# Seams of a transformer kernel: weight buffers 2/5/5, six feed-forward and five output layers in halves, state space preparation one layer on, other counts for the norm steps

## The chip, the cores and the metric

The kernel runs on one core of one Trainium2 chip. The metric is the device time of one execution in microseconds (us). The engines are PE (TensorE, matmuls), DVE (VectorE), ACT (ScalarE), POOL (GpSimd) and SP (SyncE, which here only issues DMAs). Each engine executes its own instructions in the order written for it, and waits at an instruction until the data and the buffer of that instruction are ready.

## The reference, cut to what matters

Two residual blocks over x of 512 tokens and 1024 features, in fp32, follow one another. Each sublayer starts with a root mean square norm; in the first block each ends with one, too.

```
for layer in range(2):                                     # first block
    hf = swiglu(rms_norm(x, g[0]), w_gate0, w_up0, w_down0)      # ffn0, ffn2
    x = x + 0.5 * rms_norm(hf, g[1])
    xn = rms_norm(x, g[2])
    mix = attn_mixer(xn) if layer == 0 else mlstm_mixer(xn)      # attention, mLSTM
    x = x + rms_norm(mix, g[3])
    hf = swiglu(rms_norm(x, g[4]), w_gate1, w_up1, w_down1)      # ffn1, ffn3
    x = x + 0.5 * rms_norm(hf, g[5])
x = x + even_mixer(rms_norm(x, even_norm))                 # pooling + state space (S5)
x = x + odd_mixer(rms_norm(x, odd_norm))                   # gated convolution of 31 taps
return rms_norm(x, final_norm)

rms_norm(x, g) = x * rsqrt(mean(x * x) + 1e-6) * g
swiglu(x)      = (silu(x @ w_gate) * (x @ w_up)) @ w_down  # 1024 -> 2 x 2816 -> 1024
```

The state space part of the even mixer needs exp(ssm_log_dt), powers of exp(a * dt) and tables made from them; all of that depends on weights alone, not on x.

## The kernel before, in words

x lies transposed in SBUF, as eight tiles x0 to x7 of 128 features by 512 tokens. A projection ("layer", class `Lin`) makes 128 output features: `wload` (L260) loads a 128x1024 weight tile `wt` by a DMA on SP's queue, ACT casts it to the rounded high part `wh` (L267), DVE or POOL subtracts to get the low part `wl` (L268), and `mm3` (L279) sums three matmuls for each of eight input tiles (L287 to L289: wl*xh, wh*xl, wh*xh), 24 matmuls of 512 columns for a layer. `LinTok` (L338) does the same with tokens on the rows (L354 to L356). `wt`, `wh` and `wl` have four buffers each, twelve tiles in all. The inputs are split too: `xs` holds a high part made by ACT (L433) and a low part made by DVE (L434).

A norm is not applied before a projection. The raw x (times the gain) is projected, and the result is multiplied by the factor of each token when it leaves PSUM. The factor is made on the side by `norm_factor` (L444): squares on ACT (L415), sums on POOL and DVE (L417, L419), a matmul with ones (L372) for the sum over features, a small DVE step (L391), a power on POOL (L392, the program name is `rc`, or `rsv` for a norm at a sublayer's end), and a matmul that broadcasts it (L380). These steps are a Python generator (`Chain`), and its next step is emitted after so many groups of three matmuls (`tick`, L179): the numbers that the generators yield (`lag`, 26 in `prenorm`; 6 before L380) say how many groups later.

At a seam between two sublayers the tokens are taken in two halves of 256. The last `ntail` layers of the old sublayer and the first `nfront` of the new one run on the first half and then on the second (`halves`, L316), so that norm and residual of one half (`PostNorm.chain`, L502: L508 scales, L510 reloads the residual `old` from HBM, L512 adds, then L433/L434 split and L415 to L419 square) run beside matmuls of the other. With more layers in halves than `fkeep` = `tkeep` = 4, the weights of the first ones are loaded twice. `ffn` (L516) has four front layers and two tail layers in halves; the output projections of attention (L775) and mLSTM (L1017) have three tail layers.

ffn3 carries a side job: `ssm_prep` (L1055), a generator that is stepped once after each of its undivided layers. Its first step loads ssm_log_dt into `pdt` by two broadcast DMAs (L1066), takes Exp on ACT (L1068) and loads other small arrays.

The order on each engine is made by a tile scheduler from the emitted program, priorities (`ahead`) and buffer waits, so a change of a count moves instructions on all engines.

## Time and profile before

| what | value |
|---|---|
| median of 3 runs | 2602.49 us (2600.59 to 2605.08) |
| profiled execution, its own time | 2600.32 us |
| its span, first to last instruction | 2597.8 us |
| mean granted TensorE clock | 0.982 |
| PE busy | 2469.4 us, 95% of the span, 12816 instructions |
| DVE / ACT / POOL busy | 1353.9 / 1043.9 / 645.5 us |
| HBM traffic | 101 GB/s over the span |

The sublayers follow one another: ffn0 to about 385 us, attention to 690, ffn1 to 1055, ffn2 to 1440, mLSTM to 1718, ffn3 to 2120, the even mixer to 2330, the odd mixer to 2530, the output and final norm to the end. PE's busy time is to be read with care: matmuls overlap, so the length of one (0.28 us) is not its cost; the distance between two starts is. Waits in square brackets stand at the instruction that waited, with the engine and line that released it.

### The profile page before, as it was taken

To read this page: it belongs to the slowest core of one execution; us is meant where nothing else is said; L and a number is where in the kernel's file an instruction comes from. 1 tells how busy PE (TensorE), PEld (TensorE's weight loads), DVE (VectorE), ACT (ScalarE), POOL (GpSimd) and SP (SyncE) were. 2 spreads that over 40 slices of the span, in tenths; PEclk is the share of its full clock that TensorE was granted. 3 is DMA by queue.
4 is the path that set the end of the run, shared out by engine and by line. 5 is a ranking of instruction groups with operands and counts; after the bars stand their busy time and mean duration, and the time that the engine had idled before them with its cause. 6 is when DMAs were issued, how large, how long until landed. Compare 5 with 4: busy or idle time off the path is not lost. (4 is left out here: it accounts for less than half of the span.)

```text
span 2597.8 us, 33290 instructions
## 1 busy us (share of the span) xinstructions
PE 2469.4 (95%) x12816; PEld 2071.8 (80%) x12816; DVE 1353.9 (52%) x2288; ACT 1043.9 (40%) x1778; POOL 645.5 (25%) x568
## 2 busy tenths in 40 slices
PE   8999989999999999899999899969999997999887
PEld 7888887677888888888888788868888886787677
DVE  5444246657544422644423567459963255656885
ACT  4222234446522222422223445443232247446762
POOL 2111025030311100211101253022211024317951
PEclk9999999999999999999999999989999999999998
DMA  5223335122432233422333422233433353132211
GB/s 168 96 96 93 97 103 189 49 85 66 146 104 95 95 93 106 154 98 98 95 89 102 139 97 66 86 114 126 162 131 91 95 170 136 51 121 65 65 57 49
DMA packets 99918, 268.91 MB, mean 104 GB/s; under 512 B 17280, under 2 KB 34304, under 8 KB 99248
## 3 DMA queue, kind: packets, MB, share of 16 engines
q1 hardware_dynamic: 99760, 266.79, 32.2%
q8 instruction: 101, 1.65, 0.3%
q14 instruction: 57, 0.47, 0.1%
HBM read 241.56 MB, written 20.99 MB: 101 GB/s over the span
## 5 line engine op out<-in xcount | busy, mean ns | idle before, releaser
L287 PE MATMUL pa<-xs,wl 128*128 128x512 f32 (+1 forms) x2352 | 877.8, 373 | 10.5 <-DVE wl L268 7.6
L288 PE MATMUL pa<-xs,wh 128*128 128x512 f32 (+1 forms) x2352 | 875.6, 372 | 5.1 <-DVE xs L434 5.0
L289 PE MATMUL pa<-xs,wh 128*128 128x512 f32 (+1 forms) x2352 | 872.5, 371 | 0.0
L267 ACT CAST wh<-wt 128x1024 fp32r<-128x1024 f32 (+2 forms) x423 | 432.5, 1023 | 1012.5 <-issue 602.2
L268 DVE TENSOR_TENSOR wl<-wt,wh 128x1024 fp32r<-128x1024 f32 (+2 forms) x369 | 445.7, 1210 | 456.6 <-ACT wh L267 455.5
L287 PEld LDWEIGHTS pa<-xs,wl 128*128 128x128 f32 x2352 | 445.2, 189 | 88.7 <-ACT sq L415 7.1
L288 PEld LDWEIGHTS pa<-xs,wh 128*128 128x128 f32 x2352 | 445.1, 189 | 80.4 <-DVE xs L434 7.0
L289 PEld LDWEIGHTS pa<-xs,wh 128*128 128x128 f32 x2352 | 445.0, 189 | 74.2 <-issue 1.8
L533 POOL TENSOR_TENSOR ew<-ew,rb 128x512 f32<-128x512 f32 (+1 forms) x96 | 160.5, 1673 | 711.5 <-ACT ew L532 711.5
L287 PE MATMUL pa<-hh,wl 128*128 128x512 f32 (+1 forms) x880 | 310.9, 353 | 13.7 <-DVE wl L268 13.7
L288 PE MATMUL pa<-hl,wh 128*128 128x512 f32 (+1 forms) x880 | 308.9, 351 | 0.0
L289 PE MATMUL pa<-hh,wh 128*128 128x512 f32 (+1 forms) x880 | 308.8, 351 | 0.0
L287 PEld LDWEIGHTS pa<-hh,wl 128*128 128x128 f32 x880 | 166.8, 190 | 39.0 <-DVE wl L268 14.8
L493 POOL TENSOR_TENSOR acc<-acc,ew 128x512 f32<-128x512 f32 (+1 forms) x44 | 51.0, 1159 | 546.5 <-ACT ew L488 546.5
L288 PEld LDWEIGHTS pa<-hl,wh 128*128 128x128 f32 x880 | 166.9, 190 | 24.2
L289 PEld LDWEIGHTS pa<-hh,wh 128*128 128x128 f32 x880 | 166.8, 190 | 24.1
L540 DVE TENSOR_TENSOR ew<-ew,pa 128x512 f32<-128x512 f32 (+1 forms) x96 | 61.7, 643 | 228.2 <-PE pa L289 217.0
L268 POOL TENSOR_TENSOR wl<-wt,wh 128x1024 fp32r<-128x1024 f32 x54 | 129.6, 2410 | 124.5 <-ACT wh L267 124.3
L531 DVE TENSOR_TENSOR ew<-rb,pa 128x512 f32<-128x512 f32 (+1 forms) x96 | 61.4, 642 | 176.8 <-PE pa L289 174.9
L1440 POOL TENSOR_TENSOR tp<-tp 128x512 f32<-128x512 f32 x72 | 100.0, 1389 | 5.1 <-ACT tp L1436 0.7
L1447 DVE SCALAR_TENSOR_TENSOR pc<-g,vecs,pc 128x512 f32<-128x512 f32 x120 | 85.8, 751 | 4.4 <-PE pc L1445 3.4
L488 ACT ACTIVATE ew<-pa 128x512 f32<-128x512 f32 (+1 forms) x56 | 27.4, 488 | 139.4 <-PE pa L289 139.4
(455 smaller groups left out, 2915.5 us busy)
## 6 DMA issues: line engine op xcount, KB each, us to landing
wt<-in_wgu_dram SPq DMA_DIRECT2D x176, 512.0 KB, 3.5
wt<-in_wd_dram SPq DMA_DIRECT2D x72, 512.0 KB, 3.5
wt<-in_wd_dram SPq DMA_DIRECT2D x36, 384.0 KB, 3.1
wt<-in_ow_dram SPq DMA_DIRECT2D x24, 512.0 KB, 3.2
old<-x SPq DMA_DIRECT2D x40, 256.0 KB, 3.3
old<-old SPq DMA_DIRECT2D x80, 128.0 KB, 2.5
wt<-in_aqk_dram SPq DMA_DIRECT2D x18, 512.0 KB, 4.2
wt<-in_mvo_dram SPq DMA_DIRECT2D x16, 512.0 KB, 3.6
```

The lines of the kernel that those rows point to most:

```text
L267: nc.scalar.copy(wh, wt)
L268: (eng or nc.vector).tensor_tensor(wl, wt, wh.bitcast(F32), op=ALU.subtract)
L287: mm(ps[:m, c0:c1], wl[:, j, :], xh[:, c0:c1], start=first and j == 0, stop=False)
L288: mm(ps[:m, c0:c1], wh[:, j, :], xl[:, c0:c1], start=False, stop=False)
L289: mm(ps[:m, c0:c1], wh[:, j, :], xh[:, c0:c1], start=False, stop=last and j == n - 1)
L488: nc.scalar.activation(sq[:, c0:c1], ps[:, c0:c1], AF.Square)
L493: eng.tensor_tensor(s.acc[:, c0:c1], s.acc[:, c0:c1], sq[:, c0:c1], op=ALU.add)
L531: nc.vector.tensor_tensor(s[:, c0:c1], rb[:, c0:c1], ps[:, c0:c1], op=ALU.mult)
L533: nc.gpsimd.tensor_tensor(s[:, c0:c1], s[:, c0:c1], rb[:, c0:c1], op=ALU.mult)
L540: nc.vector.tensor_tensor(s[:, c0:c1], s[:, c0:c1], ps[:, c0:c1], op=ALU.mult)
L1440: nc.gpsimd.tensor_tensor(part, part, t, op=ALU.add)
L1447: nc.vector.scalar_tensor_tensor(ps, gi[:, j:j + T], cw[:, at[j]:at[j] + 1], ps, op0=ALU.mult, op1=ALU.add)
```

## The change

Five counts and four orders change.

- `wload`: two buffers for `wt`, five each for `wh` and `wl`; still twelve tiles.
- `norm_factor`: nine groups between power and broadcast, not six. `prenorm`: lag 28 for the first half and 38 for the second, not 26.
- `ffn`: six front layers in halves, not four, in ffn1 to ffn3; two of them are loaded twice. The output projections of attention and mLSTM: five tail layers in halves, not three; one is loaded twice. That is 8 loads more (431 after 423), and 240 matmuls more (10 more layers are cut in two).
- The side job starts after the second undivided layer of ffn3, not the first; that layer is now the eighth of the sublayer.
- The first attention projections and the first value projection subtract `wl` on DVE, not POOL (8 subtracts).
- mLSTM: the gates' matmuls use the other PSUM pool, run by halves, and stand after two of the four token blocks of v; `keep_x` (the residual's copy to HBM) comes later.

```
-    wt = k.wp.tile(shape, F32, name="wt", tag="wt", bufs=4)
+    wt = k.wp.tile(shape, F32, name="wt", tag="wt", bufs=2)
...
-    wh = k.wp.tile(shape, R, name="wh", tag="wh", bufs=4)
-    wl = k.wp.tile(shape, R, name="wl", tag="wl", bufs=4)
+    wh = k.wp.tile(shape, R, name="wh", tag="wh", bufs=5)
+    wl = k.wp.tile(shape, R, name="wl", tag="wl", bufs=5)
...
-    prs = yield from rsqrt_mean(k, t, c0, c1, 1024, 1e-6, 6, v)
+    prs = yield from rsqrt_mean(k, t, c0, c1, 1024, 1e-6, 9, v)
...
-def prenorm(k, g, c0, c1, lag=26, order=range(KX)):
+def prenorm(k, g, c0, c1, lag=None, order=range(KX)):
+    lag = lag or (28 if c0 == 0 else 38)
...
-        run_lins(lins[:4], nfront=4)
+        nf = 4 if begin else 6
+        run_lins(lins[:nf], nfront=nf)
...
-                for l in lins[4:n1]:
+                for n, l in enumerate(lins[nf:n1]):
                     run_lins([l])
-                    next(work, None)
+                    if n:
+                        next(work, None)
...
-            lins = [Lin(k, [(A["aqk"][2 * a + j, i], KX)], xs, ev, nc.gpsimd) for j, ev in ((1, ev_k), (0, ev_q))]
+            eng = None if (a, i) == (0, 0) else nc.gpsimd
+            lins = [Lin(k, [(A["aqk"][2 * a + j, i], KX)], xs, ev, eng) for j, ev in ((1, ev_k), (0, ev_q))]
...
-                lin_tok(k, A["av"][0], xs, ev_v(0), nc.gpsimd)
+                lin_tok(k, A["av"][0], xs, ev_v(0))
...
-        run_lins([Lin(k, [(A["ao"][m], KX)], ys, post.evac(m)) for m in range(KX)], ntail=3, on_half=post.finish)
+        run_lins([Lin(k, [(A["ao"][m], KX)], ys, post.evac(m)) for m in range(KX)], ntail=5, on_half=post.finish)
...
-            pg = k.A_()
-            for c in HALVES:
-                mm3(k, pg, gw, xs, *c)
+            pg = k.S_()
+            mm3(k, pg, gw, xs, *HALVES[0])
+            yield
+            mm3(k, pg, gw, xs, *HALVES[1])
...
-        for tb in range(4):
+        for tb in range(2):
             lv[0].run(tb)
-        k.need("all", 0, T)
-        old = keep_x(k)
         with k.phase("mlstm_a") as pa:
             gt = gates(pa)
+            next(gt)
+            for tb in range(2, 4):
+                lv[0].run(tb)
+            k.need("all", 0, T)
+            old = keep_x(k)
             next(gt)
```

What the scheduler makes of it is shown at three places. Line numbers after the change are a little higher, by one in the norm steps (L508 is L509) up to eight from the state space on (L1068 is L1076).

**ffn0 to attention.** On DVE before, the low part `wl_2791` of a weight tile of ffn0's last layer stands between the splits xs5 and xs6 of the first half:

```order
L434 SCALAR_TENSOR_TENSOR xs4_103<-x4_95,vecs_89,xs4_103 128x256
L434 SCALAR_TENSOR_TENSOR xs5_104<-x5_96,vecs_89,xs5_104 128x256
L268 TENSOR_TENSOR wl_2791<-wt_2788,wh_2790 128x1024
L417 TENSOR_TENSOR ssq_2718<-ssq_2718,sq_2726 128x256
L434 SCALAR_TENSOR_TENSOR xs6_105<-x6_97,vecs_89,xs6_105 128x256
L417 TENSOR_TENSOR ssq_2718<-ssq_2718,sq_2729 128x256
L434 SCALAR_TENSOR_TENSOR xs7_106<-x7_98,vecs_89,xs7_106 128x256
L419 TENSOR_TENSOR ssq_2718<-ssq_2718,ssq_2710 128x256
```

and after the change it stands before the whole residual chain, right behind `wl_2785`:

```order
L268 TENSOR_TENSOR wl_2547<-wt_2544,wh_2546 128x768
L268 TENSOR_TENSOR wl_2785<-wt_2782,wh_2784 128x1024
L268 TENSOR_TENSOR wl_2791<-wt_2788,wh_2790 128x1024
L494 TENSOR_TENSOR acc_1995<-acc_1995,ew_2617 128x256
L391 TENSOR_SCALAR rsv_2636<-pb_2633 128x2
L509 TENSOR_TENSOR ew_2654<-x0_91,pb_2651 128x256
```

So this subtract moved up 24 places, ahead of the chain. On PE before, the sum over features of the second half's squares (L372 on `ssq`) comes when the first two projections (`pt`) have gone through all eight input tiles:

```order
L356 MATMUL pt<-wh,xs_106 128x512
L354 MATMUL pa<-wh,xs_99 128x512
L355 MATMUL pa<-wl,xs_99 128x512
L356 MATMUL pa<-wh,xs_99 128x512
L372 MATMUL pb<-ones,ssq 128x128 x2
L354 MATMUL pa<-wh,xs_100 128x512
L355 MATMUL pa<-wl,xs_100 128x512
```

and after it comes 30 places earlier, when the projections have only gone through the first two tiles and part of the third:

```order
L355 MATMUL pa<-wl,xs_99 128x512
L356 MATMUL pa<-wh,xs_99 128x512
L354 MATMUL pa<-wh,xs_100 128x512
L355 MATMUL pa<-wl,xs_100 128x512
L356 MATMUL pa<-wh,xs_100 128x512
L354 MATMUL pa<-wh,xs_101 128x512
L372 MATMUL pb<-ones,ssq 128x128 x2
L354 MATMUL pa<-wh,xs_99 128x512
L355 MATMUL pa<-wl,xs_99 128x512
L356 MATMUL pa<-wh,xs_99 128x512
```

The order of the two projections and of the value blocks is now mixed, tile by tile.

**ffn1 to ffn2.** On DVE before, the weights of the old sublayer's last layer (`wl_8370`) stand inside the chain of the first half:

```order
L434 SCALAR_TENSOR_TENSOR xs5_104<-x5_96,vecs_89,xs5_104 128x256
L268 TENSOR_TENSOR wl_8370<-wt_8367,wh_8369 128x1024
L417 TENSOR_TENSOR ssq_8297<-ssq_8297,sq_8305 128x256
L434 SCALAR_TENSOR_TENSOR xs6_105<-x6_97,vecs_89,xs6_105 128x256
L417 TENSOR_TENSOR ssq_8297<-ssq_8297,sq_8308 128x256
L434 SCALAR_TENSOR_TENSOR xs7_106<-x7_98,vecs_89,xs7_106 128x256
L419 TENSOR_TENSOR ssq_8297<-ssq_8297,ssq_8289 128x256
L268 TENSOR_TENSOR wl_8376<-wt_8373,wh_8375 128x768
```

and after the change, at the second half's chain of the same seam, the weights `wl_8822` and `wl_8856` of new front layers stand behind the sum of squares (L419) and the last split:

```order
L417 TENSOR_TENSOR ssq_8728<-ssq_8728,sq_8739 128x256
L434 SCALAR_TENSOR_TENSOR xs6_105<-x6_97,vecs_89,xs6_105 128x256
L419 TENSOR_TENSOR ssq_8728<-ssq_8728,ssq_8720 128x256
L434 SCALAR_TENSOR_TENSOR xs7_106<-x7_98,vecs_89,xs7_106 128x256
L541 TENSOR_TENSOR ew_8746<-ew_8746,pa_8756 128x256
L268 TENSOR_TENSOR wl_8822<-wt_8819,wh_8821 128x1024
L276 TENSOR_TENSOR hl0_8602<-ew_8746,hh0_8601 128x256
L268 TENSOR_TENSOR wl_8856<-wt_8853,wh_8855 128x1024
```

Two weight tiles that the matmuls of the front layers need now stand behind the chain.

**mLSTM to ffn3.** On ACT before, the Exp on `pdt` stands directly before the second half's squares (L415) and splits (L433), with its table load:

```order
L488 ACTIVATE ew<-pa 128x256
L489 ACTIVATE x_96<-pa,vecs 128x256
L267 CAST wh<-wt 128x1024
L1068 ACT_TABLE_LOAD
L1068 ACTIVATE pdt<-pdt 128x16
L415 ACTIVATE ssq<-x_91 128x256
L433 ACTIVATE xs_99<-x_91,vecs 128x256
L415 ACTIVATE sq<-x_92 128x256
```

and after the change the first half's broadcast factor (L451) has come ahead of it, but the squares still follow it:

```order
L489 ACTIVATE ew<-pa 128x256
L490 ACTIVATE x_94<-pa,vecs 128x256
L451 COPY rb<-pb 128x256
L267 CAST wh<-wt 128x1024 x2
L1076 ACT_TABLE_LOAD
L1076 ACTIVATE pdt<-pdt 128x16
L415 ACTIVATE ssq<-x_91 128x256
L415 ACTIVATE sq<-x_92 128x256
```

On SP's DMA queue before, the two loads of `pdt` follow five weight loads, the reload of `old` and one small load:

```order
L264 DMA wt<-in_wgu_dram 128x1024 x5
L510 DMA old<-old 128x256 x8
L1062 DMA pa__14061<-in_sa_dram 128x32
L1066 DMA pdt<-in_ldt_dram 64x16x1 x2
L1076 DMA pskip<-in_sd_dram 128x16
L1125 DMA pb__14174<-in_sb_dram 128x2x64
L264 DMA wt<-in_wgu_dram 128x1024
```

and after the change they follow six weight loads, of which two stand directly in front of them:

```order
L264 DMA wt<-in_wgu_dram 128x1024 x2
L511 DMA old<-old 128x256 x8
L264 DMA wt<-in_wgu_dram 128x1024 x2
L1070 DMA pa__14499<-in_sa_dram 128x32
L264 DMA wt<-in_wgu_dram 128x1024 x2
L1074 DMA pdt<-in_ldt_dram 64x16x1 x2
L1084 DMA pskip<-in_sd_dram 128x16
L1133 DMA pb__14613<-in_sb_dram 128x2x64
```

The loads of `pdt` thus moved behind one more weight load, and the last weight loads ahead of them need a free `wt` buffer out of two.

## Rows read from the trace of the kernel before

**Rows 1.** The page: busy time of each engine, share of the span, instructions.

```profile
PE 2469.4 (95%) x12816; PEld 2071.8 (80%) x12816; DVE 1353.9 (52%) x2288; ACT 1043.9 (40%) x1778; POOL 645.5 (25%) x568
```

**Rows 2.** Waits of PE: us in total, times, longest us.

```profile
PE pa L287 <- DVE wl L268: 24.8, 7, 7.2
...
PE pb L380 <- POOL rc L392: 24.2, 9, 18.0
...
PE pb L372 <- DVE ssq L419: 10.7, 3, 5.2
...
PE pe L1291 <- POOL xx L1284: 9.1, 3, 4.3
...
PE pt L355 <- POOL wl L268: 1.7, 1, 1.7
```

**Rows 3.** Groups and DMA issues of the page: busy us, mean ns; KB, us to landing.

```profile
L268 DVE TENSOR_TENSOR wl<-wt,wh 128x1024 fp32r<-128x1024 f32 (+2 forms) x369 | 445.7, 1210 | 456.6 <-ACT wh L267 455.5
...
L268 POOL TENSOR_TENSOR wl<-wt,wh 128x1024 fp32r<-128x1024 f32 x54 | 129.6, 2410 | 124.5 <-ACT wh L267 124.3
...
L267 ACT CAST wh<-wt 128x1024 fp32r<-128x1024 f32 (+2 forms) x423 | 432.5, 1023 | 1012.5 <-issue 602.2
...
wt<-in_wgu_dram SPq DMA_DIRECT2D x176, 512.0 KB, 3.5
```

**Rows 4.** Timeline of PE: matmuls on 256 and on 512 columns, start and length in us.

```profile
1074.06 0.28 PE L287 MATMUL pa<-xs,wl 128*128 128x256 f32 x1
...
1075.74 0.28 PE L289 MATMUL pa<-xs,wh 128*128 128x256 f32 x1
...
1199.79 0.39 PE L287 MATMUL pa<-xs,wl 128*128 128x512 f32 x1
...
1201.15 0.39 PE L287 MATMUL pa<-xs,wl 128*128 128x512 f32 x1
```

**Rows 5.** Timeline of PE, ffn0 to attention, with waits.

```profile
383.29 0.58 PE L287 MATMUL pa<-hh,wl 128*128 128x256 f32 x1 [7.02 <-DVE wl L268]
...
396.93 0.49 PE L380 MATMUL pb<-ident,rsv 128*128 128x128 f32 x2 [1.27 <-POOL rsv L392]
```

**Rows 6.** Timeline of VectorE (DVE) before the wait at 383 us.

```profile
376.97 5.13 DVE L434 SCALAR_TENSOR_TENSOR xs<-x,vecs,xs 128x256 fp32r<-128x256 f32 x2
...
382.02 1.21 DVE L268 TENSOR_TENSOR wl<-wt,wh 128x1024 fp32r<-128x1024 f32 x1
...
383.49 0.47 DVE L434 SCALAR_TENSOR_TENSOR xs<-x,vecs,xs 128x256 fp32r<-128x256 f32 x1
```

**Rows 7.** Timeline of GpSimd (POOL) beside the first row of Rows 6.

```profile
376.98 4.83 POOL L268 TENSOR_TENSOR wl<-wt,wh 128x1024 fp32r<-128x1024 f32 x2 [0.55 <-ACT wh L267]
```

**Rows 8.** Timeline of PE, ffn1 to ffn2.

```profile
1055.42 0.39 PE L287 MATMUL pa<-hh,wl 128*128 128x256 f32 x1 [3.21 <-DVE wl L268]
...
1078.21 0.68 PE L372 MATMUL pb<-ones,ssq 128*128 128x128 f32 x4 [2.20 <-DVE ssq L419]
```

**Rows 9.** Timeline of VectorE, first and last of the second half's chain.

```profile
1067.06 0.75 DVE L508 TENSOR_TENSOR ew<-x,pb 128x256 f32<-128x256 f32 x2 [1.58 <-PE pb L380]
...
1077.65 0.42 DVE L419 TENSOR_TENSOR ssq<-ssq 128x256 f32<-128x256 f32 x1
```

**Rows 10.** Timeline of PE, mLSTM to ffn3.

```profile
1730.74 0.28 PE L289 MATMUL pa<-xs,wh 128*128 128x256 f32 x1
...
1749.05 1.22 PE L380 MATMUL pb<-ident,rc 128*128 128x128 f32 x4 [18.03 <-POOL rc L392]
```

**Rows 11.** Timeline of ScalarE (ACT) in that wait.

```profile
1737.66 1.28 ACT L1068 ACT_TABLE_LOAD   x1 [17.90 <-DMA pdt<-in_ldt_dram]
```

**Rows 12.** Tile pdt: its DMAs, and their time to landing.

```profile
L1066 SPq DMA_DIRECT2D pdt<-in_ldt_dram x2: 653/664/674, 1715.2 to 1715.9; - x2
...
DMA to landing us min/median/max: 12.5/17.1/21.7
```

**Rows 13.** Window after that wait: us, busy of each engine, PEclk, DMA share, GB/s.

```profile
1749.00:1755.00 6.00, 5.89 (x32) 5.60 (x33) 4.29 (x27) 3.54 (x8) 2.38 (x4) 0.64 0.44 137
```

More of the change, by code (lines that the diff above doesn't have):

```diff
@@ L572, in ffn @@
         else:
-            run_lins(lins[4:n1])
+            run_lins(lins[nf:n1])
         pb = late.enter_context(k.phase("ffn_b"))
@@ L1016, in mlstm @@
         post = PostNorm(k, k.vec(9), old)
-        run_lins([Lin(k, [(A["mo"][m], KX)], ys, post.evac(m)) for m in range(KX)], ntail=3, on_half=post.finish)
+        run_lins([Lin(k, [(A["mo"][m], KX)], ys, post.evac(m)) for m in range(KX)], ntail=5, on_half=post.finish)
 def cmul(nc, tmp, o_re, o_im, ar, ai, br, bi, eng=None, sub=None):
```

## The prediction

> **What bounds the kernel now.** I read the busy times of the page first. PE is busy for 2469 of 2597.8 us [rows 1], so the other engines matter only where PE waits for them. The list of PE's waits comes next, and it shows where that is: 24.8 us for weight low parts in 7 waits, 24.2 us for norm factors (one wait alone has 18.0), 10.7 us for sums of squares, 9.1 us for the rotation in the even mixer [rows 2]. Nearly all of these stand at seams, where one sublayer's norm chain and the next one's first weights meet. Third come the timelines of PE around each such wait, and of the engine named as its releaser. The change is about these seams alone; inside the sublayers the order on PE stays as it is or nearly so. The forecast is therefore a sum over seams: which wait goes, and what is late next.
>
> **Prices.** A weight subtract takes 1.21 us on DVE and 2.41 on POOL, a cast 1.02 on ACT, and a 512 KB weight load lands 3.5 us after issue [rows 3]. A matmul on 256 columns takes 0.120 us start to start ((1075.74 - 1074.06) / 14), one on 512 columns 0.227 ((1201.15 - 1199.79) / 6) [rows 4]. A layer cut in halves thus costs 48 x 0.120 - 24 x 0.227 = 0.3 us more than a whole one. Ten more are cut: +3.0 us on PE, which I book at their seams, 0.6 for each pair. Eight more loads of 3.5 us lie beside 5.4 us layers and cost nothing by themselves; if a buffer is late they cost as in the second rival.
>
> **The change part by part,** in the order of the program, after minus before.
>
> *ffn0 to attention: -6.* PE waits 7.0 us at 383.29 for a weight low part [rows 5], because DVE has this subtract behind two splits (L434) of 5.13 us together, where another split takes 0.47 [rows 6]. POOL runs two weight subtracts in the same 5 us [rows 7]. After the change the subtract stands ahead of the chain, so the 7.0 goes. The mixed order of the first projections also covers the 1.27 us at 396.93 [rows 5] and the 1.7 us wait for a POOL subtract [rows 2]: 10.0 in all. But the sum of squares of the second half is now asked for 30 matmuls earlier, 30 x 0.227 = 6.8 us. The chain of a half takes 11 us (below), of which I find some 3.4 uncovered by following both queues: -10.0 + 3.4, rounded to -6. If all the covers hold it is -9; if the chain keeps the slow splits (5.13 - 2 x 0.47 = 4.2 us longer), about -2.
>
> A rule of the Trainium skill bears on this place (SBUF — State Buffer, "Who interferes with whom"): a VectorE instruction with two inputs in SBUF and a GpSimd instruction that reads SBUF shut each other out, and the one that starts first holds the shared ports to its end. The trace agrees here, with 5.13 us for two splits beside 4.83 us of POOL subtracts [rows 6, 7]. By this rule moving the subtracts to DVE takes 4.2 us of blocking out of the chain and puts 2.4 us of subtracts in, so the seam would come out 1.8 us better than my -6; I leave it inside the bounds, since the subtracts also stand in the chain's queue.
>
> *Attention to ffn1: +1.2.* Four more layers in halves; the waits of this seam are for the same chain and stay. Bounds -4 (chain hidden by the longer run in halves) to +4 (two reloads late by one 3.5 us landing).
>
> *ffn1 to ffn2: +2.3.* The 3.21 us wait at 1055.42 [rows 8] goes, since that subtract now stands before the chain. The second half's chain lasts from 1067.06 to 1078.07, 11 us [rows 9], and PE waits 2.20 us for its end at 1078.21 [rows 8]. After the change only two half layers, not three to four, stand between, one half layer (24 x 0.120 = 2.9) less: I get a wait of 4.85, that is +2.65. Then `wl_8822`, which stands behind the chain on DVE, is late by a subtract (1.2 and the step to PE: 1.4), and the next weight by some 0.8. With 0.6 for two layers in halves: -3.2 + 2.65 + 1.4 + 0.8 + 0.6. Bounds -3 (the weights are ready) to +6 (each of four weights behind the chain late by 1.2 more).
>
> *ffn2 to mLSTM: +0.6.* The longest wait for a sum of squares, 5.2 us [rows 2], turns into one for the last split of about 7.2, since the gates' matmuls now come early and ask for the second half; the factors come 1.4 earlier, and 0 to 0.6 are lost behind a cast on ACT that came between table loads. No more is lost than one chain's end, so bounds -3 to +4.
>
> *mLSTM to ffn3: +1.4.* This is the big wait: PE's last matmul before it starts at 1730.74, and the next comes at 1749.05 [rows 10]. It is put down to POOL's `rc`, but POOL and DVE had waited themselves: ACT stood 17.9 us at the Exp of the side job, until 1737.66, for `pdt` [rows 11]. Its two loads of 4 KB, issued at 1715.2 and 1715.9, took 12.5 and 21.7 us to land [rows 12], and all squares and splits of the second half are behind that Exp on ACT. After the change five tail layers let the first factor come 5.8 us earlier and get past the Exp. The squares of the second half do not: the Exp still stands ahead of them. And the loads of `pdt` are now behind one more weight load on SP's queue, which has to wait for one of only two `wt` buffers; I find their issue at about 1722, 6.5 us later, and landing at 1722 + 21.7 = 1744. Eight squares and the sums follow in 6 us, to 1750. PE has four half layers until about 1734.6 in the meantime, and then waits some 15 us instead of 18. But eleven layers are cut in halves at this seam instead of seven, +1.2, and the end of the front comes out at 1776.5 where it was 1775.1. So the change doesn't do here what the moved side job seems to offer. Bounds -10 (first rival) to +8 (`pdt` another 6.5 late).
>
> The Trainium skill (DMA: Bandwidth & Descriptors, "Rules for kernel authors") has a rule against this part: issue a DMA early and wait for it late, and a last dimension that is not contiguous costs a descriptor for each element. The trace agrees, with 21.7 us for 4 KB beside 3.5 us for 512 KB [rows 3, 12]. By the rule the later issue alone would cost the whole 6.5; by the queues above, 5.8 of it is paid back by the earlier factor.
>
> *ffn3 to even: -1.6.* A wait for a weight of 2.2 us, one of the seven [rows 2], goes as in ffn1 to ffn2, less 0.6 for halves already counted in the front. Bounds -3 to 0.
>
> *Even mixer: +2.4.* Before the last pair of rotations POOL now has one more weight subtract in its queue, 2.41 us [rows 3], and PE waits for that rotation already (4.3 us at most [rows 2]). Bounds 0 to 4.8, for none and two.
>
> *Start, odd mixer, output: -1.* At the start the factor comes 3 groups later, and PE has other half layers there (-0.5); the output has four layers to start on where it had three (-0.7); bounds -3 to +2.
>
> Sum: -6 + 1.2 + 2.3 + 0.6 + 1.4 - 1.6 + 2.4 - 1 = -0.7. The profiled execution took 2600.3 us, 2.5 around its span, and lies 2.2 below the median. On that scale I expect 2599.6, on the scale of the median 2602.5 - 0.7 = 2601.8.
>
> **The rivals.**
> First, the 18 us wait goes after all. For it: the factor of the first half does get past the Exp, and the two loads may land in 12.5 us each when less traffic surrounds them. Against it: the Exp's place ahead of the squares. Then PE waits perhaps 5 us for the 11 us chain in place of 18, and the restart is spared as well: in the 6 us after the wait the granted clock was 0.64 [rows 13], between the two levels of 1.2 and 2.4 GHz, a loss of 0.36 x 6 = 2.2 us. -13 - 2.2 gives 2587.
>
> Second, slower: two `wt` buffers starve the halves. A buffer is held for landing, cast and subtract, 3.5 + 1.02 + 1.21 = 5.7 us [rows 3], so two buffers give a weight each 2.9 us, while a half layer takes 2.9 us on PE. There is no slack, and one subtract that is held up behind a chain delays all that follow. It decides once a subtract comes over 3 us late; then each of five seams loses some 2 us more: +10, 2612. Against it: whole layers of 5.4 us win it back, and the converted `wl` and `wh` have one buffer more.
>
> Third, faster at several seams without touching the big wait: the attention seam gives all of its -9, and the weights behind the chains are ready in time (-3 and -3 at the feed-forward seams, 0 in the even mixer): some -9, 2593. For it: 24.8 us of waits for weights is the largest sum in the list. Against it: what stands next in the queues is the 11 us chain, and it is not shorter.
>
> **How the numbers follow.** Forecast as it stands (2596 to 2607): 0.41. First rival 0.16, second 0.22, third 0.21. A measurement of this kernel can tell 0.2%, 5.2 us, from no change. The first and third rival are faster, 0.37; the forecast is the same, 0.41; the second is slower, 0.22. The range from 2586 to 2613 takes in all three rivals' middles and leaves out their far ends.
>
> **What would show it.** Right: the wait of 7 us at 383 is gone and a wait for `ssq` of 3 to 4 us stands in its place; after ffn1 a wait for `ssq` of nearly 5 us, then short ones for `wl`; ACT still waits some 20 us for `pdt`, and PE some 15 in two pieces. Wrong: no wait over 8 us left between 1700 and 1770 (first rival), or a row of `wl` waits of 1 to 3 us after each seam (second).

## The result, and the profile after

The changed kernel took 2624.36 us (median of 4 runs, 2621.32 to 2626.22), the kernel before 2602.09 us beside it: a ratio of 1.0083, 95% interval 1.0066 to 1.0100. It is slower by 22 us, where I had forecast no change (2601.8) and a range to 2613. The profiled execution has a span of 2624.2 us, 26.4 more than before's, and is one of the two slower of its four.

The page's busy times of the changed kernel, as in [rows 1]:

```profile
PE 2476.8 (94%) x13056; PEld 2087.2 (80%) x13056; DVE 1369.7 (52%) x2313; ACT 1055.2 (40%) x1802; POOL 640.5 (24%) x567
```

PE has 7.4 us more work, from 240 matmuls more and from matmuls at a lower clock. The other 19 us are waits. PE's waits in the changed kernel (total, times, longest), as in [rows 2]:

```profile
PE pb L372 <- DVE ssq L419: 17.5, 8, 6.7
PE pa L287 <- DVE ew L532: 17.4, 1, 17.4
PE pe L1299 <- POOL xx L1289: 11.3, 1, 11.3
PE pa L287 <- DVE wl L268: 11.0, 4, 7.2
PE pa L287 <- ACT x L490: 10.3, 3, 4.8
...
PE pa L354 <- DVE vx L876: 6.6, 1, 6.6
...
PE pb L380 <- POOL rc L392: 5.9, 5, 1.9
```

The 24.8 us for weight low parts are down to 11.0, as forecast. But the waits for sums of squares grew from 10.7 to 17.5, a wait of 17.4 us stands where 18.0 stood, under another name (it ends with a split's `ew`, no more with `rc`), and three are new or grown: 11.3 us for one rotation in the even mixer, 10.3 for ACT's copies (L490), 6.6 for a split of v (the L876 row).

Where the time came from is read by the start of the same matmul in both timelines, for instance the first down projection of each feed-forward sublayer, the first and last score matmul of attention, the first pooling matmul of the even mixer. The stretches between them, changed minus before:

| stretch | forecast | measured |
|---|---|---|
| ffn0 to attention | -6 | -3.1 |
| attention to ffn1 | +1.2 | +2.0 |
| ffn1 to ffn2 | +2.3 | +6.4 |
| ffn2 to mLSTM | +0.6 | +3.6 |
| mLSTM to ffn3 | +1.4 | +8.9 |
| ffn3 to even mixer, rotations | +0.8 | +11.6 |
| all the rest | -1 | -3.0 |
| sum | -0.7 | +26.4 |

A measured row is the difference of two single traces, and the granted clock of a stretch differs from execution to execution: in two runs below, c_rest and c_444_lags, PE's waits from ffn0 to attention are the same 6.5 us, and the stretch is 3.8 us apart, with a granted clock of 0.96 and 0.99. So a difference of less than some 4 us between two stretches is not read as a cause unless the waits show it, too.

Three stretches carry it. **The even mixer**: POOL's, ACT's, DVE's and PE's timelines around the third rotation of the changed kernel.

```profile
2214.23 2.40 POOL L268 TENSOR_TENSOR wl<-wt,wh 128x1024 fp32r<-128x1024 f32 x1 [11.28 <-ACT wh L267]
2222.25 4.67 POOL L268 TENSOR_TENSOR wl<-wt,wh 128x1024 fp32r<-128x1024 f32 x2 [5.62 <-ACT wh L267]
2226.87 1.26 POOL L1279 TENSOR_TENSOR r<-r,r 128x512 f32<-128x512 f32 x1
```

```profile
2214.71 6.39 ACT L1303 COPY yf<-pe 32x128 f32<-32x128 f32 x16
2221.12 1.05 ACT L267 CAST wh<-wt 128x1024 fp32r<-128x1024 f32 x1
```

```profile
2213.77 0.68 DVE L1281 TENSOR_TENSOR r<-pe,rot 128x512 f32<-128x512 f32 x1
2228.16 2.27 DVE L1285 TENSOR_TENSOR_SCAN r<-rot,r 128x512 f32<-128x512 f32 x1 [13.71 <-POOL r L1279]
```

```profile
2236.31 0.79 PE L1299 MATMUL pe<-xx,mt 128*128 128x127 f32 x2 [11.26 <-POOL xx L1289]
2241.11 0.80 PE L1299 MATMUL pe<-xx,mt 128*128 128x127 f32 x2 [4.01 <-POOL xx L1292]
```

DVE's products are ready at 2214.4. POOL's addition (L1279) comes at 2226.87, 12.4 us later, since three weight subtracts (7.1 us together) stand ahead of it and the second waits 5.62 us for its cast. (The first one's wait of 11.28 us is over at 2214.23, just before the products are ready.) The cast at 2221.12 in turn stands behind 16 copies of 6.39 us on ACT. PE waits 11.26 and then 4.01 us.

The kernel before waited for its rotations, too: 9.1 us [rows 2], and 3.8 us in this row of the same list.

```profile
PE pe L1291 <- POOL xx L1281: 3.8, 2, 2.0
```

So 15.3 us in two long waits stand in place of 12.9 in five, 2.4 us more. All of PE's waits in this stretch are 31.1 us, 20.3 before: of the other 8.4 us, the input splits have 3.4, ACT's copies to `u` 3.1 and POOL's weights 2.2.

**mLSTM to ffn3**: SP's queue, ACT and PE, as in [rows 10 to 12].

```profile
1731.09 2.08 SPq L264 DMA_DIRECT2D wt<-in_wgu_dram  x2
1733.22 1.39 SPq L1074 DMA_DIRECT2D pdt<-in_ldt_dram  x2
```

```profile
1756.84 1.28 ACT L1076 ACT_TABLE_LOAD   x1 [18.52 <-DMA pdt<-in_ldt_dram]
```

```profile
1763.30 0.58 PE L287 MATMUL pa<-xs,wl 128*128 128x256 f32 x1 [17.44 <-DVE ew L532]
```

The loads of `pdt` go out at 1733.22, right behind two weight loads; the Exp on ACT waits 18.52 us for them until 1756.84, and PE 17.44 us until 1763.30. And ahead of that a wait that the kernel before doesn't have, ACT and PE:

```profile
1718.22 1.29 ACT L433 ACTIVATE xs<-x,vecs 128x256 fp32r<-128x256 f32 x3
...
1719.41 0.36 ACT L489 ACTIVATE ew<-pa 128x256 f32<-128x256 f32 x1
```

```profile
1720.19 0.58 PE L287 MATMUL pa<-yh,wl 128*128 128x256 f32 x1 [4.79 <-ACT x L490]
```

PE has finished a tail layer's second half and needs its PSUM bank, but ACT copies it out (L489, L490) only after the squares and splits of the first half, from 1719.41 on.

**ffn1 to ffn2**: PE at the second half's sum of squares, and the windows behind it and behind the waits of 4.79 and 17.44 us above (length, busy of each engine, PEclk, DMA share, GB/s).

```profile
1077.55 1.19 PE L372 MATMUL pb<-ones,ssq 128*128 128x128 f32 x4 [6.72 <-DVE ssq L419]
```

```profile
1077.40:1082.00 4.60, 3.88 (x16) 3.61 (x17) 3.40 (x6) 0.41 (x1) 0.71 (x1) 0.50 0.64 196
1082.00:1087.00 5.00, 5.00 (x33) 5.00 (x32) 2.09 (x4) 2.40 (x3) 0.00 (x0) 0.69 0.34 103
1720.70:1725.00 4.30, 4.30 (x28) 4.30 (x27) 4.30 (x9) 1.77 (x6) 0.97 (x2) 0.69 0.21 61
1763.30:1768.00 4.70, 4.70 (x23) 4.70 (x24) 4.70 (x11) 4.67 (x11) 1.63 (x1) 0.53 0.97 351
```

The wait is 6.72 us, where [rows 8] have 2.20. In the 4.6 us behind it the clock was granted at 0.50, that is at the lower of its two levels, and at 0.69 in the next 5; behind the waits of 4.79 and 17.44 us shown above it was 0.69 and 0.53. In the same place of the kernel before, behind its wait of 2.2 us, it was full:

```profile
1078.10:1083.00 4.90, 4.74 (x38) 4.61 (x39) 2.90 (x9) 2.23 (x6) 2.12 (x3) 1.00 0.37 107
```

So by my estimate from these rows the long wait costs up to another 4.6 x 0.50 + 5 x 0.31 = 3.9 us.

### The profile page after: what moved, and what is told of

The parts are those of the page before. It is cut to its first block, busy times and chain, and to the rows that moved or that the text cites. A ratio compares the mean times of both kernels' runs of the same rounds, so it can differ in the third digit from the quotient of the medians.

```text
span 2624.2 us, 33843 instructions
## 1 busy us (share of the span) xinstructions
PE 2476.8 (94%) x13056; PEld 2087.2 (80%) x13056; DVE 1369.7 (52%) x2313; ACT 1055.2 (40%) x1802; POOL 640.5 (24%) x567
## 5 line engine op out<-in xcount | busy, mean ns | idle before, releaser
L287 PE MATMUL pa<-xs,wl 128*128 128x512 f32 (+1 forms) x2408 | 889.2, 369 | 35.8 <-DVE ew L532 17.4
L288 PE MATMUL pa<-xs,wh 128*128 128x512 f32 (+1 forms) x2408 | 884.5, 367 | 0.4 <-DVE xs L434 0.4
L289 PE MATMUL pa<-xs,wh 128*128 128x512 f32 (+1 forms) x2408 | 882.0, 366 | 0.0
L267 ACT CAST wh<-wt 128x1024 fp32r<-128x1024 f32 (+2 forms) x431 | 440.8, 1023 | 1053.4 <-issue 485.3
L268 DVE TENSOR_TENSOR wl<-wt,wh 128x1024 fp32r<-128x1024 f32 (+2 forms) x385 | 465.1, 1209 | 466.7 <-ACT wh L267 465.9
L287 PEld LDWEIGHTS pa<-xs,wl 128*128 128x128 f32 x2408 | 458.9, 191 | 111.0 <-DVE ew L532 17.6
L289 PEld LDWEIGHTS pa<-xs,wh 128*128 128x128 f32 x2408 | 458.6, 190 | 72.1 <-issue 2.0
L288 PEld LDWEIGHTS pa<-xs,wh 128*128 128x128 f32 x2408 | 458.9, 191 | 71.6 <-ACT wh L267 1.0
L287 PEld LDWEIGHTS pa<-hh,wl 128*128 128x128 f32 x880 | 165.4, 188 | 24.2
L268 POOL TENSOR_TENSOR wl<-wt,wh 128x1024 fp32r<-128x1024 f32 x46 | 111.0, 2418 | 148.8 <-ACT wh L267 148.6
L489 ACT ACTIVATE ew<-pa 128x256 f32<-128x256 f32 (+1 forms) x60 | 28.0, 466 | 136.4 <-PE pa L289 136.4
```

The lines of the kernel that those rows point to most:

```text
L267: nc.scalar.copy(wh, wt)
L268: (eng or nc.vector).tensor_tensor(wl, wt, wh.bitcast(F32), op=ALU.subtract)
L287: mm(ps[:m, c0:c1], wl[:, j, :], xh[:, c0:c1], start=first and j == 0, stop=False)
L288: mm(ps[:m, c0:c1], wh[:, j, :], xl[:, c0:c1], start=False, stop=False)
L289: mm(ps[:m, c0:c1], wh[:, j, :], xh[:, c0:c1], start=False, stop=last and j == n - 1)
L489: nc.scalar.activation(sq[:, c0:c1], ps[:, c0:c1], AF.Square)
```

## The experiments

"Before" is run beside each, at 2601 to 2603 us. The number after a time is its ratio to "before", and all intervals are 95%. Names such as a_444 are those of the runs; what a stretch gains or loses is given against the kernel before, as in the table above.

**One part of the change undone.** The buffers at 4/4/4:

```
-    wt = k.wp.tile(shape, F32, name="wt", tag="wt", bufs=2)
+    wt = k.wp.tile(shape, F32, name="wt", tag="wt", bufs=4)
-    wh = k.wp.tile(shape, R, name="wh", tag="wh", bufs=5)       (and wl)
+    wh = k.wp.tile(shape, R, name="wh", tag="wh", bufs=4)       (and wl)
```

> The changed kernel with four buffers each for wt, wh and wl again (all other edits stay). Theory: two wt buffers hold back the two weight loads that stand in front of the pdt loads on SP's queue; with four the pdt loads go out near 1722 us instead of 1733, so the stretch from mLSTM to ffn3 gets some 8 us back. The even mixer keeps its loss, since the order on POOL there is the same (four weight subtracts between the second and the third rotation): its segment from ffn3's first down projection to the first pooling matmul stays at 255.7 us within 3. Total about 2614. Rival (the buffers are the cause of all of it): every seam goes back to before, total 2602 to 2605. Second rival (buffers cost nothing): 2624.

Measured (a_444): 2618.34, ratio 1.0063 (1.0048 to 1.0078). Six us come back, but not where I said: the loads of `pdt` do go out earlier, at 1726.0 in place of 1733.2, but PE still waits 18.8 us there and mLSTM to ffn3 stays at +9.3. The even mixer goes from +11.6 to +4.7, and PE's waits in it from 31.1 to 22.4 us. With four buffers two subtracts, as in the kernel before, and no longer four, stand between the second and the third rotation, and POOL adds at once behind them, 4.5 us after DVE's products:

```profile
2209.66 2.39 POOL L268 TENSOR_TENSOR wl<-wt,wh 128x1024 fp32r<-128x1024 f32 x1 [8.73 <-ACT wh L267]
2217.78 2.40 POOL L268 TENSOR_TENSOR wl<-wt,wh 128x1024 fp32r<-128x1024 f32 x1 [5.73 <-ACT wh L267]
2220.14 1.29 POOL L1279 TENSOR_TENSOR r<-r,r 128x512 f32<-128x512 f32 x1
```

The counts of the norm steps:

```
-    prs = yield from rsqrt_mean(k, t, c0, c1, 1024, 1e-6, 9, v)
+    prs = yield from rsqrt_mean(k, t, c0, c1, 1024, 1e-6, 6, v)
-    lag = lag or (28 if c0 == 0 else 38)
+    lag = lag or 26
```

> The changed kernel with the old counts of the norm steps (26 for both halves, 6 before the broadcast), everything else as changed, two wt buffers too. Theory: the counts set the order in the even mixer; with the old ones three weight subtracts stand on POOL before the third rotation in place of four, and the wait of 11.3 us there falls to about 5, some -7; at ffn1 to ffn2 the second sum of squares is asked for later, some -2. Total about 2615. Rival (buffers alone): no change, 2624 within 3.

Measured (a_lags): 2626.26, 1.0098 (1.0083 to 1.0113). No gain in all: the wait of 11.3 us fell to 3.1, but one of 5.2 for ACT's copies came ahead of it, and what ffn2 to mLSTM gained (8 us) ffn0 to attention and attention lost.

Three tail layers in halves, and four front layers (each alone):

```
-        run_lins([Lin(k, [(A["mo"][m], KX)], ... ntail=5, on_half=post.finish)     (A["ao"] too)
+        run_lins([Lin(k, [(A["mo"][m], KX)], ... ntail=3, on_half=post.finish)
...
-        nf = 4 if begin else 6
+        nf = 4
```

> The changed kernel with three tail layers in halves at the output projections of attention and mLSTM. Theory: the two new waits of PE for ACT's copies of a tail layer (4.7 us at 675, 4.8 us at 1720, L490 behind the first half's squares and splits on ACT) come from the five layers in halves and go; the segment to ffn1 falls by some 2 and that to ffn3 by some 4 (less halves 1.2 too); total 2618. Rival: the first half's chain is then uncovered instead and its factor later, no gain or some 4 us of loss.

Measured (b_ntail3): 2620.46, 1.0069 (1.0054 to 1.0084): 4 us. By the traces 2.8 lie at mLSTM to ffn3 and 2.9 in the even mixer, and attention to ffn1 lost 2.7; each is small enough to be the clock of one execution.

> The changed kernel with four front layers in halves in ffn1 to ffn3. Theory: the wait of 6.7 us for the second sum of squares at 1077 comes from the counts and not from the number of front layers, so it stays, and only 0.6 us for each of three seams comes back: 2622. Rival (six layers in halves with two wt buffers starve PE): ffn1 to ffn2 gets 3 to 6 us back and the other seams some 2, total below 2616.

Measured (b_nf4): 2617.12, 1.0056 (1.0041 to 1.0071). The wait for the sum of squares stays (6.4 us), as the theory said, but 7 us come back: 4.3 in the even mixer (1.9 of them in PE's waits), 3.1 at mLSTM to ffn3 (a wait of 2.8 us inside ffn3, for a state space table, is gone), 2.3 at ffn1 to ffn2.

**One part of the change alone.** The kernel before with 2/5/5, with 2/4/4 and with 3/4/4. In these three the edit also gave the same number, 2 or 3 in place of 4, to a tile of attention that has the same name (L703), a part that the change doesn't have:

```
-    wt = k.wp.tile(shape, F32, name="wt", tag="wt", bufs=4)
+    wt = k.wp.tile(shape, F32, name="wt", tag="wt", bufs=2)
-    wh = k.wp.tile(shape, R, name="wh", tag="wh", bufs=4)       (and wl)
+    wh = k.wp.tile(shape, R, name="wh", tag="wh", bufs=5)       (and wl)
...
-            wt = pool.tile([P, T], F32, name="wt", tag="wt", bufs=4)
+            wt = pool.tile([P, T], F32, name="wt", tag="wt", bufs=2)
```

> The kernel before with buffers 2/5/5 and nothing else. Theory: two wt buffers by themselves bring a weight late wherever the next load waits for a subtract that stands in a long queue; the even mixer loses some 7 (as 4/4/4 gave 7 back there in the changed kernel), the start of ffn3 0 to 3; total 2609 to 2612. Rival (the loss needs the halves and the counts too): 2602 within 3.

Measured (b_255): 2624.43, 1.0084 (1.0067 to 1.0101).

> The kernel before with two wt buffers, wh and wl at four as before. Theory: the loss of buffers 2/5/5 comes from the two wt buffers, since a load for the next sublayer can't be issued before an old subtract behind the norm chain is done; the five wh and wl give little back: 2622 to 2630. Rival (the fifth wh and wl changed the order on the engines and did the harm): below 2610.

Measured (c_b244): 2635.26, 1.0126 (1.0109 to 1.0144).

> The kernel before with three wt buffers, wh and wl at four. Theory: the price is that of a load that can't be issued until an old subtract behind the norm chain is done; with three buffers one more load is ahead, and of the 33 us of 2/4/4 less than 8 are left: 2602 to 2610. Rival (each buffer costs alike, half of it is left): 2618.

Measured (d_b344): 2609.73, 1.0031 (1.0017 to 1.0045).

Then 2/5/5 and 2/4/4 again, for the weights alone:

> The kernel before with the weights' buffers alone at 2/5/5. b_255 had one line more in it than meant: attention's probability tile, which is also called wt, went from 4 buffers to 2, a part that the change does not have. In its trace that shows as +4.0 us inside attention, and part of the +3.8 ahead of it and the +3.0 behind it may come from there too. Theory (the weights' buffers carry the seams): inside attention within 1 us of before; ffn1 to ffn2 still +6 and ffn3 to even mixer still +8; ratio 1.0065 (2619), that is 5 us less than b_255. Rival (the attention tile was most of it): ratio 1.003 (2610) or below, and ffn1 to ffn2 under +3.

Measured (e_255): 2623.18, 1.0093 (1.0079 to 1.0107).

> The kernel before with the weight tile wt alone at 2 buffers, wh and wl at 4: c_b244 without the attention tile that went to 2 buffers there as well. Theory: 5 to 6 us less than c_b244, 2629 (1.0105), so that the fifth wh and wl stay worth some 10 us. Rival: the fifth wh and wl only mend what the attention tile upset; then no more than 2 us apart from e_255.

Measured (e_244): 2633.08, 1.0124 (1.0110 to 1.0138). The tile of attention cost nothing clear of noise in either (ratios of 1.0084 and 1.0093 with and without it, 1.0126 and 1.0124); both prices that I gave it were wrong, and the 3.8 us inside attention, which I had laid at its door, are there without it. So the weight buffers alone cost all of the 22 us, double my theory for b_255; the fifth `wh` and `wl` are worth 10, and a third `wt` gives back 26 of the 33 us (both with the attention tile cut as well). How a load comes to be late is seen on SP at ffn1 to ffn2. First the kernel before, then e_255, then DVE of e_255:

```profile
1032.23 3.64 SPq L264 DMA_DIRECT2D wt<-in_wgu_dram  x2
1045.17 8.28 SPq L510 DMA_DIRECT2D old<-old  x8
```

```profile
1050.88 0.33 SPq L264 DMA_DIRECT2D wt<-in_wgu_dram  x1
1059.23 8.28 SPq L510 DMA_DIRECT2D old<-old  x8
1071.04 7.74 SPq L264 DMA_DIRECT2D wt<-in_wgu_dram  x4
```

```profile
1070.02 0.94 DVE L268 TENSOR_TENSOR wl<-wt,wh 128x768 fp32r<-128x768 f32 x1
...
1070.96 1.20 DVE L268 TENSOR_TENSOR wl<-wt,wh 128x1024 fp32r<-128x1024 f32 x1
```

Before, two weight loads of ffn2 go out 13 and 11 us ahead of the reload of the residual (`old`). With two buffers it is one, 8 us ahead; the second goes out at 1071.04, 12 us behind the start of the reload and thus some 23 us later than before. It goes out only when DVE, at the end of the norm chain, does the subtracts that hold the two buffers (1070.02 and 1070.96).

PE, however, does not wait longer for weights. Its waits in e_255, as in [rows 2] (the one named `identr` is the wait for the first weight of all, which [rows 2] have under `wl`, 7.2 us):

```profile
PE pb L380 <- POOL rc L392: 33.0, 10, 19.1
PE pb L372 <- DVE ssq L419: 17.7, 7, 4.4
...
PE pa L287 <- DVE identr L243: 6.9, 1, 6.9
...
PE pa L287 <- DVE wl L268: 4.0, 2, 3.1
```

The waits for DVE's low parts fell from 24.8 to 10.9 us; those for factors rose from 24.2 to 33.0 and those for sums of squares from 10.7 to 17.7. At ffn1 to ffn2, too, PE waits 0.9 us for weights (3.2 before) and 6.4 for two sums of squares (2.2 before); 24 matmuls more than before stand between the second sum and ffn2's down projection, and the granted clock is 0.50 in the 4.5 us after it. That the late load moved these matmuls is likely, but no run shows it.

One place shows the way from a late load to another wait: the start of the even mixer, +9.0 in e_255. ACT and PE of e_255, then PE of the kernel before:

```profile
2160.07 1.04 ACT L267 CAST wh<-wt 128x1024 fp32r<-128x1024 f32 x1 [1.14 <-DMA wt<-in_ew_dram]
2161.14 13.96 ACT L1250 COPY u<-yf 32x128 f32<-32x128 f32 x32
```

```profile
2157.81 0.71 PE L380 MATMUL pb<-ident,rc 128*128 128x128 f32 x4 [1.03 <-POOL rc L392]
2162.94 1.22 PE L1261 MATMUL pe<-u,mt 128*128 128x128 f32 x4 [4.42 <-ACT u L1250]
```

```profile
2143.75 0.71 PE L380 MATMUL pb<-ident,rc 128*128 128x128 f32 x4 [1.04 <-POOL rc L392]
2146.08 0.80 PE L287 MATMUL pa<-xs,wl 128*128 128x512 f32 x1 [1.61 <-POOL wl L268]
```

A cast waits for its weight, and the copies to `u` behind it on ACT begin at 2161.14, 3.3 us after PE's broadcast (2157.81). In the kernel before they begin 1.6 us after it, and PE has a projection to run in the meantime (2146.08). With two buffers none stands there, and PE waits 4.42 us for `u`.

**Without the buffers' part.** From the changed kernel with 4/4/4, the halves and counts are taken back, too:

```
+        ... ntail=3, on_half=post.finish)                   (c_444_ntail3, c_rest)
+    lag = lag or 26, and 6 before the broadcast             (c_444_lags, c_rest)
+        nf = 4                                              (c_rest)
```

The names behind the lines are the runs that have this edit.

> The changed kernel with four buffers each and three tail layers in halves. Theory: with four buffers the remaining 16 us of loss are mostly from the halves; the segments attention to ffn1 (+7.0 with four buffers) and mLSTM to ffn3 (+9.3) go back by 4 and 5: 2609. Rival (the counts of the norm steps do it): 2617 within 3.

Measured (c_444_ntail3): 2605.60 (10 runs, 2599 to 2611), 1.0011 (1.0000 to 1.0022). With four buffers, five tail layers were 13 of the 16 us.

> The changed kernel with four buffers each and the old counts of the norm steps. Theory: the counts matter at ffn1 to ffn2, ffn2 to mLSTM and the even mixer (+4.8, +2.6, +4.7 with four buffers), together some -7, and ffn0 to attention gives 4 back: 2614. Rival (the counts are the cause of the remaining loss): below 2606.

Measured (c_444_lags): 2617.30, 1.0052 (1.0033 to 1.0071): the counts are worth 1 us.

> What is left of the change without the buffers, the halves and the counts: first attention projections subtracted on DVE, the gates of mLSTM in halves after two blocks, the side job one layer on. Theory: ffn0 to attention keeps its gain of 3 to 5, the gates cost or win 2, and mLSTM to ffn3 goes back to the 18 us wait: 2599 within 3. Rival (the gates or the side job carry a loss of their own): over 2606.

Measured (c_rest): 2601.91 (10 runs), 1.0000 (0.9990 to 1.0010). The edits that are left are worth nothing.

**The waits themselves.** The load of ssm_log_dt, first in the changed kernel, then in the one before:

```
-    ld = A["ldt"].rearrange("(q two) -> two q", two=2)
-    for gg in range(2):
-        nc.sync.dma_start(dt[gg * 64:(gg + 1) * 64, :], ld[gg:gg + 1, :].to_broadcast([64, 16]))
+    dt2 = pool.tile([P, 16, 2], F32, name="pdt2")
+    nc.sync.dma_start(dt2.rearrange("p q two -> p (q two)"),
+                      A["ldt"].rearrange("(o f) -> o f", o=1).to_broadcast([P, 32]))
...
-    nc.scalar.activation(dt, dt, AF.Exp)
+    for gg in range(2):
+        h = slice(gg * 64, (gg + 1) * 64)
+        nc.scalar.activation(dt[h], dt2[h, :, gg], AF.Exp)
```

> The changed kernel with ssm_log_dt loaded by one DMA of 32 contiguous values to each of 128 partitions, in place of two with 16 values at a stride of two, at the same place in SP's queue; the even and odd values are picked when Exp reads them. Theory: the time to landing falls from 23 us to about 3, ACT waits until about 1738 instead of 1757, and PE's wait of 17.4 us at 1763 goes down to under 5: total some -13, 2611. Rival (the second half's chain or SP's queue is the limit, and the landing is hidden): the wait stays over 12 us, total over 2620.

Measured (a_pdt): 2603.36 (10 runs), 1.0009 (1.0000 to 1.0019): 21 us back. The time to landing of `pdt`:

```profile
DMA to landing us min/median/max: 3.4/3.4/3.4
```

It lands 3.4 us after issue, and the longest wait of PE between 1700 and 1770 is now the 4.6 us for ACT's copies.

> The kernel before with ssm_log_dt loaded by one DMA of contiguous rows, nothing else. Theory: ACT waits for pdt only until about 1720 instead of 1737.7, so PE's wait of 18.0 us at 1749 falls to about 3: 2586. Rival (the second half's chain takes the place of the wait): half of that, 2594.

Measured (b_before_pdt): 2581.95, 0.9921 (0.9906 to 0.9936), 20 us faster than the kernel before. The longest wait for a factor fell from 18.0 [rows 2] to 1.3:

```profile
DMA to landing us min/median/max: 3.0/3.0/3.0
```

```profile
PE pb L380 <- POOL rc L392: 7.3, 11, 1.3
```

The even mixer's subtracts on DVE:

```
-        gp = nc.gpsimd
+        gp = None
```

> The changed kernel with the weight subtracts of the even mixer's z and pooling layers on DVE instead of POOL. Theory: the third rotation stands behind four subtracts on POOL, of which each waits for a cast on ACT; without them POOL adds as soon as DVE has multiplied, and the two waits of 11.3 and 4.0 us of PE in the even mixer fall below 5 together: -10 or more, 2612. Rival (the weights are late because of two wt buffers, wherever they are subtracted): PE waits for weights instead, less than 3 us gained.

Measured (a_evdve): 2613.06, 1.0047 (1.0032 to 1.0062): 11 us back, all in the even mixer (+11.6 falls to +1.1, PE's waits in it from 31.1 to 22.7 us).

**Both together, on three bases:** the contiguous load and the even mixer's subtracts on DVE, first in the kernel before, then in the kernel of c_rest, then in that of c_444_ntail3.

> The kernel before with the contiguous load of ssm_log_dt and with the even mixer's weight subtracts on DVE. Theory: the load gave 20 us, the subtracts on DVE gave 10.5 in the changed kernel's even mixer, of which the kernel before had lost 12.6 in its four waits for the rotation; 2582 - 6 = 2576. Rival (the wait there is the chain of rotations itself): 2582.

Measured (d_best1): 2581.20, 0.9920 (0.9905 to 0.9934). That is what the load gave alone: in the kernel before, the subtracts on POOL cost nothing that DVE wouldn't cost.

> As the run before, with the first attention projections subtracted on DVE, the new gates and the moved side job, with four buffers, four front and three tail layers and the old counts. Theory: these edits were worth nothing together (c_rest), so 2576 within 4. Rival (they cover a wait that the 18 us hid): 2570.

Measured (d_best_rest): 2584.01, 0.9930 (0.9915 to 0.9944).

> The same with the new counts of the norm steps and six front layers in halves. Theory: ffn0 to attention gives 5 us, ffn1 to ffn2 and mLSTM take 4 back: 2575. Rival (the halved front covers more once the load of ssm_log_dt is quick): 2568.

Measured (d_best_nt3): 2586.09, 0.9938 (0.9923 to 0.9953). The gain of 6.7 us at ffn0 to attention is there, but mLSTM to ffn3 gives back 8 of the 18.

So the version that beats both kernels is the kernel before with the contiguous load alone, 2582; none of the parts of the change that were tried on top adds to it.

## Why the prediction was wrong

**The step that failed** is "eight more loads ... cost nothing by themselves; if a buffer is late they cost as in the second rival", and with it the price of that rival. I walked the new order of each engine, but took the two `wt` buffers into account at one place only (the loads in front of `pdt`) and priced their case at +10, with a chance of 0.22. By itself this part cost 22 us (e_255). The rival named the right part, a buffer held for landing, cast and subtract with no slack, but its price was half of that, and the sign that it gave, "a row of `wl` waits of 1 to 3 us after each seam", did not come: with the buffers alone PE's waits for DVE's low parts fell. What I missed is, first, where the subtract stands: at a seam it is behind the 11 us chain on DVE or behind rotations on POOL, and the next sublayer's second load goes out 23 us later than with four buffers. And second, who pays: the work that stands behind a late cast on ACT and behind a late subtract on POOL, and PE, which has a layer less to run in the meantime. The start of the even mixer shows this; for the other seams it is argued.

**The five tail layers** were booked as a gain (the first factor 5.8 us earlier) at +1.2 for the halves. They cost 13 us with four buffers, and 4 with the changed ones. The shown part is the wait for ACT's copies behind the chain of the first half: 4.8 us at mLSTM and 4.7 at attention in the changed kernel, 4.6 and 5.5 with four buffers; with three tail layers and four buffers (c_444_ntail3) no wait for these copies is over 0.8. The wait behind `pdt` is 18.8 us with five and 15.3 with three. I had followed DVE's and POOL's queue behind the chain, and ACT's only for the Exp. The two traces differ by 3.5 us at ffn1 to ffn2 and 4.0 in the even mixer as well, far from any tail layer of the output projections. In the even mixer that is the clock: PE's waits are the same (22.4 and 22.5 us), and the granted clock is 0.95 and 0.97 over some 245 us. At ffn1 to ffn2 the waits differ by 1.1 us, and by what the rest comes about, no run shows. The trace of c_444_ntail3 is the fastest of its ten runs.

**The sizes do not add up,** and the sum over seams supposed that they would: buffers alone 22, the rest alone 16, both 22. It shows most from attention to ffn1: PE's waits there are 6.0 us before, 10.6 with the buffers alone, 10.1 with the rest alone and 7.7 with both. So no single part is the cause of the 22 us; why the two losses hide each other, no run shows.

Step by step. *ffn0 to attention*: the 7.0 us wait went, as forecast; the new waits are 1.48, 2.05 and 2.08 us, 5.6 in place of the 3.4 that I had booked, and -6 (-10.0 + 3.4 is -6.6) became -3.1.

```profile
380.27 0.68 PE L372 MATMUL pb<-ones,ssq 128*128 128x128 f32 x4 [1.48 <-DVE ssq L419]
...
397.94 0.50 PE L354 MATMUL pa<-wh,xs 128*128 128x512 f32 x1 [2.05 <-DVE ew L660]
...
402.53 1.20 PE L372 MATMUL pb<-ones,ssq 128*128 128x128 f32 x4 [2.08 <-DVE ssq L419]
```

The slow splits went too: in the changed kernel each takes 0.96 us at most around there, with no POOL subtract beside it, which agrees with what the Trainium skill says (SBUF — State Buffer, "Who interferes with whom").

```profile
377.37 0.96 DVE L434 SCALAR_TENSOR_TENSOR xs<-x,vecs,xs 128x256 fp32r<-128x256 f32 x1
...
378.58 0.47 DVE L434 SCALAR_TENSOR_TENSOR xs<-x,vecs,xs 128x256 fp32r<-128x256 f32 x1
```

*ffn1 to ffn2*: right in kind (a longer wait for the second sum of squares). It was 6.7 us, not 4.85 (2.20 + 2.9 is 5.1), and I priced it by its length alone; the up to 3.9 us at the lower clock behind it were left out. The 2.2 us booked for late weights behind it were 0.6. *ffn2 to mLSTM*: the wait for the split came as said, 6.6 us against 7.2, again with a clock of 0.50 behind it. *mLSTM to ffn3*: the Exp kept its place, and `pdt` came nearly when I said: 1733.2 and 1756.8 less the 10.3 us by which mLSTM ended late are 1722.9 and 1746.5, against 1722 and 1744. But PE waited 17.4 us for what is behind it and not some 15, and I lacked the copies' wait (+3.1 net of the old one there) and 2.8 us inside ffn3. *Even mixer*: one more subtract on POOL was priced at its own 2.41 us. Between the second and the third rotation there are two more, four in place of two, and one of them waits for its cast behind 16 copies on ACT: the addition comes 12.4 us after its products, where with four buffers it is 4.5. Even so the waits for rotations grew by only 2.4 us in all. That this is the size booked is luck, since one wait of 11.3 took the place of several short ones. What the sum left out are the other waits of the stretch, 8.4 us more; with +0.8 forecast and +11.6 measured it is the largest miss of the seven.

*The rivals*: the first did not come true; the Exp kept its place ahead of the squares, as its counterargument said. That taking its cause away is worth 20 us, and not 13 to 15, a_pdt and b_before_pdt show. The Trainium skill's rule there (DMA: Bandwidth & Descriptors, "Rules for kernel authors": rearrange a last dimension that is not contiguous) fits what the runs show: the two strided loads landed 12.5 and 21.7 us after their issue [rows 12], the contiguous one 3.0. The edit also makes one load of two, and no run tells the two effects apart. The third rival is summed wrongly: with the other terms as they stand, its own add up to -12.8 and 2590, not to -9 and 2593.

## What to carry to other kernels

Count for each buffer not how long its own load, cast and subtract take, but what stands in front of the last of them in its engine's queue where the queue is longest: that is how far ahead the next load can go out. Then look for the loss not only in waits for weights, but in whatever stands behind the late cast and subtract on their engines. When an instruction is moved in front of another on an engine, price the wait that it brings along, not its duration. And look first at what the longest wait is for; here one line (a load with a stride) was worth 20 us in both kernels, as much as the whole change took.

## What the runs showed of the hardware

A wait on PE has a tail. In the 4 to 5 us behind waits of 4.79, 6.72 and 17.44 us the granted clock was 0.69, 0.50 and 0.53, and behind one of 2.20 us it stayed at 1.00 (windows above). So where a change makes some waits longer and others shorter, their lengths alone are a poor price.

Two loads of 4 KB, whose 4-byte values lie at a stride of two, landed 12.5 and 21.7 us after their issue [rows 12]. The same 32 values as one contiguous row for each of 128 partitions landed after 3.0 to 3.4 us.
